# Chunk 0 of a state space scan moved in front of the last two blocks of an input projection

## The chip, the cores and the metric

One core of a Trainium2 chip runs the whole kernel in one launch. The metric is the device time of one execution in microseconds (us). Engines are named as in the profile: PE is TensorE's matmul, PEld its weight load, DVE VectorE, ACT ScalarE, POOL GpSimd, SP SyncE, whose queue issues all the DMAs here.

## The reference

One decoder block on 1024 tokens of width 1024, in float32:

```
h    = LN(x)
proj = h @ w_in                      # 5648 columns: xs 1024, z 1024, B 256, C 256, dt 16, glu 2048, cgate 1024
xbc  = silu(causal conv of width 4 over (xs, B, C));   dt = softplus(dt + bias)
y    = ssd(xs, dt, B, C) + d_skip * xs                 # 16 heads of 64, 2 groups, state 128, chunks of 128 tokens
yz   = y * silu(z);   y_ssm  = yz * rsqrt(mean(yz^2) per group) * norm_g
u    = glu_a * sigmoid(glu_b);  u = silu(LN(causal conv of width 31 over u));  y_conf = u * silu(cgate)
h    = LN(alpha * h + concat(y_ssm, y_conf) @ w_out + b_out)
out  = LN(alpha * h + sigmoid(h @ w_gate) * (p @ w_ple))
```

In the scan, each chunk of 128 tokens has a part within the chunk, (C B^T masked and decayed) times (dt * xs), and from chunk 1 on a part that reads the state left by the chunks before it, C times state. Then the state is decayed and the chunk's own B^T (decayed dt * xs) is added.

## The kernel before, in words

All large products are done as three products of two-part numbers (a rounded high part and the rest), accumulated in one PSUM bank: `three`, L122 to 125. A weight or activation is split in two by `split` (L117): ACT casts the high part, another engine (mostly POOL) subtracts it for the low part.

The input projection works in blocks of 128 output columns: `inproj` (L188) makes 48 products of 128x512 for a block, 24 a half, into banks "ps" of the PSUM tag "s" (three banks), each half emptied by ACT. The blocks come in the order: dt, B, C and xs beside the conformer's glu blocks (L624 to 633), then z blocks (`z_tile`, L384, output `zt`, stored to `z_d`), then eight gate blocks (`gate_tile`, L294, output `cg`), whose results are multiplied into the conformer's `accs` and stored to `mix_d`; the last two z blocks, z6 and z7, stand behind them (LAST_Z = 2, L636 to 641).

`prep(c)` (L441) prepares a chunk: it loads `xb` (xs, B and C of the chunk), the decay rows `gt` twice and `ea`, takes 16 exps on ACT, transposes xs on PE (`xtok`) for `xdt` (DVE) and `xdd` (ACT), transposes B and forms C B^T (`bps`), masks it (`cbm`) and multiplies it into the decay (L477). `chunk(c)` (L485) makes `yo` (C times state, not for chunk 0), `yd` (the part within the chunk), adds the skip into `y` on DVE, multiplies by `sz` (silu of z, loaded from `z_d` by `z_load`), stores `y_d`, and moves the state on with `sp` (L514 to 521). `mean_square(c)` (L524) squares `y` into the buffer of `ea` and sums it (`pr`). `conf_out(c)` (L548) is the conformer half of the output projection for the chunk's 128 tokens: 48 products into two banks "pso" (tag "o"), in the order of the weights wc[0] to wc[7], with the two parts `mH`, `mL` that `mix_load(c)` made. The weights `wc` are loaded and split by `out_weight` (L419): raw `wor`, high part `woh`, low part `wol`; wc[3] and wc[7] put `wor` in a "y" buffer (L644). The other half of the output projection (`out_proj`, "pss") and the gate (`gate`, "psg") follow for all chunks at the end.

Buffers are shared by tag: "xb" 2, "gt" 4, "u" 2, "xd" 2, "y" 2, "ha" 3, "st" 1 (L67), and areas "W" 8, "E" 4, "M" 4, which hold the two parts of h (`hH`, `hL`) until the last block of the input projection has read them. In code order the "y" buffers go to cg of gate blocks 0, 1, 6, 7, to zt of z6 and z7, to wor of wc[3] and wc[7], then to y of chunk 0, 1 and so on; the "xb" buffers to xb(0), mraw of mix_load(0), xb(1), xb(2).

The order on each engine's queue is not written by hand. The framework's planner fixes it before the run from the order of the code, the dependences, the buffers and its own estimate of each instruction's time; the engines then run their queues in that order, each waiting for semaphores.

The part around the change, before:

```
ready = [prep(0)]                                        # L635
while len(others) > LAST_Z: others.pop(0)()              # z2 to z5
for j in range(NK): gate_tile(j, CG_TAGS[j])             # gate blocks 0 to 7
for f in others: f()                                     # z6, z7
wc = [...]; mix = [mix_load(0)]; szs = [z_load(0)]       # L644
ready.append(prep(1)); szs.append(z_load(1))
for c in range(NT):                                      # L650
    done = chunk(c, szs.pop(0), *ready.pop(0))
    ...                                                  # prep(c + 2), mean_square(c), mix_load(c + 1), conf_out(c)
```

Of the kernel before, what the change touches and what calls it, by code (L numbers as in the profile page):

```python
# [15 lines left out]
L = 1024  # L16
# [30 lines left out]
def tile_block(ctx: ExitStack, tc: tile.TileContext, x, pT, wple, win, wdt, wout, wgate, vec, rows, heads, out):  # L47
# [22 lines left out]
    def work(name, tag, n=L):  # L70
        return wk.tile([P, SIZE.get(tag, L)], F32, name=name, tag=tag, bufs=BUFS[tag])[:, 0:n]

    def slabs(a, n=NK):
        return a.rearrange("p (k l) -> p k l", k=n)

    def bank(name):
        return pp.tile([P, 512], F32, name=name, tag="s", bufs=3)
# [68 lines left out]
    def area(name, tag):  # L146
        return regA.tile([P, L], F32, name=name, tag=tag, bufs={"W": 8, "E": 4, "M": 4}[tag])
# [146 lines left out]
    def gate_tile(j, tag):  # L294
        cg = work("cg", tag)
        inproj(T_CG + j, lambda hs, ps: nc.scalar.activation(out=cg[:, hs], in_=ps, func=AF.Silu))
        nc.scalar.activation(out=accs[j], in_=accs[j], func=AF.Silu, scale=v("clg", j), bias=v("clb", j))
        nc.vector.tensor_tensor(out=accs[j], in0=accs[j], in1=cg, op=ALU.mult)
        nc.sync.dma_start(out=mix_d[:, :, j, :].rearrange("t p l -> p t l"), in_=by_chunk(accs[j]))
# [141 lines left out]
    def prep(c):  # L441

        xb = slabs(work("xb", "xb", 12 * P), 12)
        nc.sync.dma_start(out=xb, in_=xbc_d[c])
        gg = []
        for g in range(2):
            gt = slabs(work("gt", "gt"))
            r0 = c * HEADS + g * 8
            nc.sync.dma_start(out=gt, in_=acs_d[r0:r0 + 8, :].unsqueeze(0).broadcast_to([P, 8, P]))
            gg.append(gt)  # L450
        ea = slabs(work("ea", "u") if c == 0 else area("ea", "E"))
        for q in range(2):
            er = ea_d[c * HEADS:(c + 1) * HEADS, :].rearrange("(t q) l -> q t l", q=2)[q]
            nc.sync.dma_start(out=ea[q * HD:(q + 1) * HD], in_=er.unsqueeze(0).broadcast_to([HD, NK, P]))

        for h in range(HEADS):
            sl = gg[h // 8][:, h % 8, :]
            nc.scalar.activation(out=sl, in_=sl, func=AF.Exp, bias=col(nacs, c, h))
        xdt = work("xdt", "xd")
        xt = pair("xtok")  # L460
        for t in range(NK):
            nc.tensor.transpose(out=xt[:, t * P:(t + 1) * P], in_=xb[:, t, :], identity=ident)
        nc.vector.tensor_tensor(out=heads3(xdt), in0=heads3(xt), in1=col(dtok, c, 0, HEADS).unsqueeze(2).broadcast_to([P, HEADS, HD]), op=ALU.mult)
        xdd = work("xdd", "u") if c == 0 else area("xdd", "E")
        for h in range(HEADS):
            nc.scalar.activation(out=xdd[:, h * HD:(h + 1) * HD], in_=xdt[:, h * HD:(h + 1) * HD], func=AF.Copy, scale=col(dec, c, h))
        bps = bbank("bps")
        for g in range(2):
            nc.tensor.transpose(out=bps[:, g * P:(g + 1) * P], in_=xb[:, 8 + g, :], identity=ident)
            mm(bps[:, (2 + g) * P:(3 + g) * P], lhsT=xb[:, 8 + g, :], rhs=xb[:, 10 + g, :], start=True, stop=True)  # L470
        btok = wk.tile([P, 2 * P], F32, name="btok", tag="btok")
        nc.scalar.copy(out=btok, in_=bps[:, 0:2 * P])
        cbm = wk.tile([P, 2, P], F32, name="cbm", tag="cbm", bufs=1)
        nc.vector.tensor_tensor(out=cbm, in0=bps[:, 2 * P:4 * P].rearrange("p (g l) -> p g l", g=2),
                                in1=tri.unsqueeze(1).broadcast_to([P, 2, P]), op=ALU.mult)
        for g in range(2):
            nc.vector.scalar_tensor_tensor(out=gg[g], in0=gg[g], scalar=1.0, in1=cbm[:, g:g + 1, :].broadcast_to([P, 8, P]), op0=ALU.min, op1=ALU.mult)  # L477
        return xb, gg, ea, xdt, xdd, btok

    def z_load(c):  # L480
        sz = slabs(work("sz", "xd" if c == 0 else "u"))
        nc.sync.dma_start(out=sz, in_=z_d[c])
        return sz

    def chunk(c, sz, xb, gg, ea, xdt, xdd, btok):  # L485
        y = slabs(work("y", "y"))
        for g in range(2):

            ys = y[:, g * 4:g * 4 + 4, :]
            es = ea[:, g * 4:g * 4 + 4, :]  # L490
            if c:
                yo = bank("yo")
                for t in range(4):
                    j = g * 4 + t
                    mm(yo[:, t * P:(t + 1) * P], lhsT=state[:, j * P:(j + 1) * P], rhs=xb[:, 10 + g, :], start=True, stop=True)
                nc.vector.tensor_tensor(out=es, in0=slabs(yo, 4), in1=es, op=ALU.mult)
            yd = bank("yd")
            for h in range(8):
                q = h % 2
                t = h // 2  # L500
                hh = g * 8 + h
                mm(yd[q * HD:(q + 1) * HD, t * P:(t + 1) * P], lhsT=xdt[:, hh * HD:(hh + 1) * HD], rhs=gg[g][:, h, :], start=True, stop=True)
            for t in range(4):
                j = g * 4 + t
                nc.vector.scalar_tensor_tensor(out=y[:, j, :], in0=xb[:, j, :], scalar=v("dsk", j), in1=yd[:, t * P:(t + 1) * P], op0=ALU.mult, op1=ALU.add)
            if c:
                nc.gpsimd.tensor_tensor(out=ys, in0=ys, in1=es, op=ALU.add)
        nc.gpsimd.tensor_tensor(out=y, in0=y, in1=sz, op=ALU.mult)
        nc.sync.dma_start(out=y_d[c], in_=y)
        if c + 1 < NT:  # L510
            if c:
                nc.gpsimd.tensor_tensor(out=heads3(state), in0=heads3(state),
                                        in1=col(cdec, c, 0, HEADS).unsqueeze(2).broadcast_to([P, HEADS, HD]), op=ALU.mult)
            for g in range(2):  # L514
                sp = bank("sp")
                gs = slice(g * 512, g * 512 + 512)
                mm(sp, lhsT=btok[:, g * P:(g + 1) * P], rhs=xdd[:, gs], start=True, stop=True)
                if c:
                    nc.vector.tensor_tensor(out=state[:, gs], in0=state[:, gs], in1=sp, op=ALU.add)
                else:  # L520
                    nc.vector.tensor_copy(out=state[:, gs], in_=sp)
        return y, ea

    def mean_square(c, y, ea):  # L524

        sq = ea.rearrange("p (g t) l -> p g t l", g=2)
        nc.scalar.activation(out=sq, in_=y.rearrange("p (g t) l -> p g t l", g=2), func=AF.Square)
        nc.gpsimd.tensor_tensor(out=sq[:, :, 0:2, :], in0=sq[:, :, 0:2, :], in1=sq[:, :, 2:4, :], op=ALU.add)
        nc.gpsimd.tensor_tensor(out=sq[:, :, 0, :], in0=sq[:, :, 0, :], in1=sq[:, :, 1, :], op=ALU.add)
        pr = bbank("pr")  # L530
        for g in range(2):
            mm(pr[:, g:g + 1], lhsT=sq[:, g, 0, :], rhs=inv512[:, 0:1], start=True, stop=True)
        rsm = const.tile([P, 2], F32, name=f"rsm{c}")
        vem = small("vem", 2)
        nc.vector.tensor_scalar(out=vem, in0=pr[:, 0:2], scalar1=EPS, scalar2=None, op0=ALU.add)
        nc.gpsimd.tensor_tensor(out=rsm, in0=vem, in1=mhalf[:, 0:2], op=ALU.pow)
        rss.append(rsm)

    def mix_load(c):
        raw = slabs(work("mraw", "xb", L) if c == 0 else area("mraw", "M"))  # L540
        nc.sync.dma_start(out=raw, in_=mix_d[c])
        ha = work("ha", "ha")
        nc.sync.dma_start(out=ha, in_=ha_d[c])
        mH, mL = slabs(area("mH", "M")), slabs(area("mL", "M"))
        split(raw, mH, mL, nc.gpsimd if c else nc.vector)
        return mH.bitcast(F32R), mL.bitcast(F32R), ha
# [88 lines left out]
    ready = [prep(0)]  # L635
    while len(others) > LAST_Z:  # L636
        others.pop(0)()
    for j in range(NK):
        gate_tile(j, CG_TAGS[j])
    for f in others:  # L640
        f()

# [1 line left out]
    wc = [out_weight(wout[NK + k], *regs[k], "y" if k % 4 == 3 else None) for k in range(NK)]  # L644
    mix = [mix_load(0)]
    szs = [z_load(0)]
    ready.append(prep(1))
    szs.append(z_load(1))
    ws = []
    for c in range(NT):  # L650
        done = chunk(c, szs.pop(0), *ready.pop(0))
        if c + 2 < NT:
            ready.append(prep(c + 2))
            szs.append(z_load(c + 2))
        mean_square(c, *done)
        if c + 1 < NT:
            mix.append(mix_load(c + 1))
        conf_out(c, *mix.pop(0))
        if c < 3:
            ws.append(out_weight(wout[c], area, "W", None, v("sng", c)))  # L660
# [72 lines left out]
```

## Time and profile before

| | us |
|---|---|
| median of 3 runs (lowest, highest) | 900.91 (900.71, 906.92) |
| the profiled execution | 904.0 |
| its span, first to last instruction | 902.3 |

The profile is that of the one profiled execution; times in it count from the first instruction. Its mean granted TensorE clock is 0.994 of full. Times of rows are us unless marked ns; L12 is line 12 of the kernel. A busy time of PE is modelled at its end, so the number of products in a stretch says more than their durations do.

### The profile page before, as it was taken

The page shows a single profiled execution, that of the slowest core. Times are in us where ns is not written, and L with a number is a line of the kernel's source. Part 1 is how long each engine was busy: PE and PEld are TensorE (multiplying, and loading weights), DVE is VectorE, ACT ScalarE, POOL GpSimd, SP SyncE. Part 2 cuts the span into 40 slices and gives each one's busy share as a digit, 9 for nine tenths or more (in the row PEclk, how much of TensorE's full clock was granted, in tenths as well). Part 3 has the DMA queues.
Part 4 walks back from the last instruction along what each step waited for, and adds up shares of the span by engine and source line. Part 5 has one row for each costly group of instructions (what it writes and reads, how often), then busy time and mean ns, then how long its engine had stood idle before and what let it go on. Part 6 is the DMA issues. An engine that isn't in the chain of part 4 may idle for free. (4 is left out here: it accounts for less than half of the span.)

```text
span 902.3 us, 11012 instructions
## 1 busy us (share of the span) xinstructions
PE 866.7 (96%) x4141; PEld 705.7 (78%) x4141; DVE 638.4 (71%) x738; ACT 393.5 (44%) x649; POOL 515.2 (57%) x298
## 2 busy tenths in 40 slices
PE   6989999999999999999999999999999889999995
PEld 4757888888888888888788887777877668888885
DVE  7968993799999989894414604774664876666666
ACT  4632336767334456554584536754743421111001
POOL 2559829999832299997652345666666432222211
PEclk9999999999999999999999999999999899999999
DMA  9612423121221313234241879787787702222211
GB/s 339 252 44 97 176 84 117 30 94 46 94 84 58 94 46 129 70 94 117 70 141 47 249 232 338 268 305 224 250 274 262 291 24 94 94 94 93 71 47 70
DMA packets 67716, 126.42 MB, mean 140 GB/s; under 512 B 4176, under 2 KB 41552, under 8 KB 67664
## 3 DMA queue, kind: packets, MB, share of 16 engines
q1 hardware_dynamic: 67664, 125.73, 41.5%
q8 instruction: 32, 0.52, 0.2%
q14 instruction: 20, 0.16, 0.1%
HBM read 89.93 MB, written 35.78 MB: 139 GB/s over the span
## 5 line engine op out<-in xcount | busy, mean ns | idle before, releaser
L123 PE MATMUL ps<-hH,wl 128*128 128x512 f32 x704 | 274.4, 391 | 2.5 <-DVE hH L177 2.5
L124 PE MATMUL ps<-hL,wh 128*128 128x512 f32 x704 | 274.8, 391 | 1.1 <-DVE hL L179 1.1
L125 PE MATMUL ps<-hH,wh 128*128 128x512 f32 x704 | 274.3, 390 | 0.0
L291 DVE SCALAR_TENSOR_TENSOR pc<-u,vc,pc 128x1024 f32<-128x1024 f32 x174 | 223.7, 1285 | 3.5
L286 POOL TENSOR_TENSOR acc<-acc,prod 128x1024 f32<-128x1024 f32 x60 | 146.1, 2435 | 18.1 <-ACT acc L282 15.3
L123 PEld LDWEIGHTS ps<-hH,wl 128*128 128x128 f32 x704 | 131.9, 188 | 29.8 <-DVE hH L177 3.0
L124 PEld LDWEIGHTS ps<-hL,wh 128*128 128x128 f32 x704 | 132.3, 188 | 28.9 <-DVE hL L179 1.5
L125 PEld LDWEIGHTS ps<-hH,wh 128*128 128x128 f32 x704 | 132.3, 188 | 27.4 <-issue 0.2
L120 POOL TENSOR_TENSOR wl<-wraw,wh 128x1024 fp32r<-128x1024 f32 x44 | 110.2, 2504 | 72.6 <-PE ps L123 39.1
L132 POOL TENSOR_SCALAR ve<-mv 128x1 f32<-128x1 f32 x24 | 22.2, 926 | 122.1 <-DVE mv L612 86.9
L285 ACT ACTIVATE prod<-u,vc 128x1024 f32<-128x1024 f32 x60 | 69.0, 1153 | 46.8 <-POOL acc L286 36.7
L119 ACT CAST wh<-wraw 128x1024 fp32r<-128x1024 f32 x44 | 46.2, 1049 | 67.8 <-DMA wraw<-in_win_dram 42.5
L380 DVE SCALAR_TENSOR_TENSOR pc<-xin,vc,pc 128x512 f32<-128x512 f32 x72 | 53.5, 747 | 5.9 <-ACT pc L247 3.4
L123 PE MATMUL pss<-woh,yL 128*128 128x512 f32 x128 | 51.7, 404 | 5.7 <-DVE r L581 3.5
L123 PE MATMUL pso<-woh,mL 128*128 128x512 f32 x128 | 51.8, 407 | 2.9 <-POOL mL L120 1.9
L123 PE MATMUL psg<-woh,hTL 128*128 128x512 f32 (+1 forms) x136 | 52.3, 385 | 1.1 <-DVE hTL L120 1.1
L125 PE MATMUL psg<-woh,hTH 128*128 128x512 f32 (+1 forms) x136 | 52.0, 382 | 0.0
L125 PE MATMUL pso<-woh,mH 128*128 128x512 f32 x128 | 51.9, 407 | 0.0
L124 PE MATMUL pso<-wol,mH 128*128 128x512 f32 x128 | 51.7, 404 | 0.0
L124 PE MATMUL psg<-wol,hTH 128*128 128x512 f32 (+1 forms) x136 | 51.6, 380 | 0.0
L124 PE MATMUL pss<-wol,yH 128*128 128x512 f32 x128 | 50.9, 398 | 0.0
L125 PE MATMUL pss<-woh,yH 128*128 128x512 f32 x128 | 50.9, 398 | 0.0
(183 smaller groups left out, 1390.4 us busy)
## 6 DMA issues: line engine op xcount, KB each, us to landing
wraw<-in_win_dram SPq DMA_DIRECT2D x44, 512.0 KB, 3.7
gt<-acs_d SPq DMA_DIRECT2D x16, 512.0 KB, 5.2
wor<-in_wout_dram SPq DMA_DIRECT2D x16, 512.0 KB, 6.8
xbc_d<-cacc SPq DMA_DIRECT2D x12, 512.0 KB, 3.4
xb<-xbc_d SPq DMA_DIRECT2D x8, 768.0 KB, 6.3
xt<-in_x_dram SPq DMA_DIRECT2D x8, 512.0 KB, 8.9
ple_d<-pl SPq DMA_DIRECT2D x8, 512.0 KB, 3.8
ha_d<-xt SPq DMA_DIRECT2D x8, 512.0 KB, 4.8
```

The lines of the kernel that those rows point to most:

```text
L119: nc.scalar.copy(out=h.bitcast(F32R), in_=src)
L120: leng.tensor_tensor(out=l.bitcast(F32R), in0=src, in1=h, op=ALU.subtract)
L123: mm(ps, lhsT=ll, rhs=rh, start=first, stop=False)
L124: mm(ps, lhsT=lh, rhs=rl, start=False, stop=False)
L125: mm(ps, lhsT=lh, rhs=rh, start=False, stop=last)
L132: eng.tensor_scalar(out=ve, in0=var, scalar1=EPS, scalar2=None, op0=ALU.add)
L285: nc.scalar.activation(out=pr, in_=u[:, i:i + L], func=AF.Copy, scale=v("ccw", j * KC + i))
L286: nc.gpsimd.tensor_tensor(out=acc, in0=acc, in1=pr, op=ALU.add)
L291: nc.vector.scalar_tensor_tensor(out=pc if i + 1 < KC else acc, in0=u[:, i:i + L], scalar=v("ccw", j * KC + i), in1=pc, op0=ALU.mult, op1= ...
L380: nc.vector.scalar_tensor_tensor(out=pc, in0=xin[:, o + j:o + j + 512], scalar=v("scw", i * 4 + j), in1=pc, op0=ALU.mult, op1=ALU.add)
```

## The change

Behind the last gate block and ahead of z6 and z7, the code now has chunk 0 up to its `y`, the state after chunk 0 (`advance(0)`) and prep(1). The gating of chunk 0 by z, its store, and all of chunk 1 on stay behind the weights `wc` in the loop. `chunk` is cut in three: `chunk` (y), `gated` (times silu of z, and the store) and `advance` (the state). The buffers move with it: `ea` of chunk 0, never read for its values, is no longer loaded, and `mean_square(0)` takes an "E" area of its own; `ea(1)` and `xdd(1)` take "u" buffers in place of "E" areas, `sz(1)` an "xd" buffer in place of a "u" one, and `mraw` of mix_load(0) a "gt" buffer in place of an "xb" one. The `y` of chunk 0 now comes ahead of zt of z6 and z7 and of wor of wc[3] and wc[7] in the order of the "y" buffers.

```diff
@@ prep @@
-        ea = slabs(work("ea", "u") if c == 0 else area("ea", "E"))
-        for q in range(2):
+        ea = slabs(work("ea", "u") if c == 1 else area("ea", "E")) if c else None
+        for q in range(2 if c else 0):
...
-        xdd = work("xdd", "u") if c == 0 else area("xdd", "E")
+        xdd = work("xdd", "u") if c < 2 else area("xdd", "E")
@@ z_load @@
-        sz = slabs(work("sz", "xd" if c == 0 else "u"))
+        sz = slabs(work("sz", "xd" if c < 2 else "u"))
@@ chunk @@
-    def chunk(c, sz, xb, gg, ea, xdt, xdd, btok):
+    def chunk(c, xb, gg, ea, xdt):
...
-            es = ea[:, g * 4:g * 4 + 4, :]
             if c:
+                es = ea[:, g * 4:g * 4 + 4, :]
...
+        return y
+
+    def gated(c, y, sz):
         nc.gpsimd.tensor_tensor(out=y, in0=y, in1=sz, op=ALU.mult)
         nc.sync.dma_start(out=y_d[c], in_=y)
+
+    def advance(c, xdd, btok):
+
         if c + 1 < NT:
...
-        return y, ea
@@ mean_square @@
+        if ea is None:
+            ea = slabs(area("sq", "E"))
@@ mix_load @@
-        raw = slabs(work("mraw", "xb", L) if c == 0 else area("mraw", "M"))
+        raw = slabs(work("mraw", "gt") if c == 0 else area("mraw", "M"))
@@ the order @@
     for j in range(NK):
         gate_tile(j, CG_TAGS[j])
+
+    y0 = chunk(0, *ready[0][0:4])
+    advance(0, *ready.pop(0)[4:])
+    ready.append(prep(1))
     for f in others:
         f()
...
     szs = [z_load(0)]
-    ready.append(prep(1))
     szs.append(z_load(1))
     ws = []
     for c in range(NT):
-        done = chunk(c, szs.pop(0), *ready.pop(0))
+        if c:
+            xb, gg, ea, xdt, *rest = ready.pop(0)
+            y = chunk(c, xb, gg, ea, xdt)
+        else:
+            y, ea = y0, None
+        gated(c, y, szs.pop(0))
+        if c:
+            advance(c, *rest)
         if c + 2 < NT:
             ready.append(prep(c + 2))
             szs.append(z_load(c + 2))
-        mean_square(c, *done)
+        mean_square(c, y, ea)
```

## Rows read from the trace of the kernel before

**Rows 1.** The page, busy us of the engines (share of the span), xinstructions.
```profile
PE 866.7 (96%) x4141; PEld 705.7 (78%) x4141; DVE 638.4 (71%) x738; ACT 393.5 (44%) x649; POOL 515.2 (57%) x298
```
**Rows 2.** Busy us by stretch: stretch, length, engines (xinstructions), PEclk, DMA share, GB/s.
```profile
521.00:543.00 22.00, 22.00 (x99) 18.19 (x97) 1.76 (x1) 7.59 (x10) 10.50 (x4) 1.00 0.69 216
...
543.00:575.00 32.00, 28.50 (x189) 22.73 (x188) 21.74 (x31) 23.82 (x61) 17.62 (x8) 1.00 0.94 309
575.00:699.00 124.00, 119.91 (x722) 95.50 (x721) 72.80 (x119) 62.62 (x182) 83.61 (x54) 1.00 0.80 266
...
688.00:699.00 11.00, 11.00 (x49) 9.09 (x50) 5.24 (x11) 4.31 (x4) 7.37 (x6) 1.00 0.87 327
...
705.00:710.00 5.00, 5.00 (x12) 3.33 (x11) 5.00 (x3) 1.04 (x1) 5.00 (x3) 0.50 1.00 366
```
**Rows 3.** Waits of PE, 543 to 699: us in total, times, longest.
```profile
PE bps L469 <- DVE cbm L474: 2.4, 1, 2.4
PE pr L532 <- POOL ea L529: 1.9, 2, 1.7
PE pso L123 <- POOL mL L120: 1.9, 1, 1.9
PE pso L123 <- DVE mL L120: 1.0, 1, 1.0
```
**Rows 4.** Timeline of PE: start, us, line, operation, tiles, count, [idle before <-releaser].
```profile
543.27 1.97 PE L502 MATMUL yd<-gt,xdt 128*64 128x128 f32 x32
545.28 1.13 PE L517 MATMUL sp<-xdd,btok 128*128 128x512 f32 x2
...
560.97 1.05 PE L495 MATMUL yo<-xb,state 128*128 128x128 f32 x8
561.86 1.04 PE L462 MATMUL xtok<-ident,xb 128*128 128x128 f32 x8
565.33 0.33 PE L469 MATMUL bps<-ident,xb 128*128 128x128 f32 x1 [2.44 <-DVE cbm L474]
...
704.53 0.79 PE L123 MATMUL pss<-woh,yL 128*128 128x512 f32 x1 [2.25 <-DVE ha L555]
```
**Rows 5.** Tile gt, 455 to 480: ns min/median/max, first and last start.
```profile
L458 ACT ACTIVATE gt<-gt,nacs x32: 384/387/405, 458.4 to 475.1; 128x128 f32<-128x128 f32 x32
```
**Rows 6.** Timeline of SP: DMA issues.
```profile
539.39 0.33 SPq L422 DMA_DIRECT2D wor<-in_wout_dram  x1
...
545.25 0.38 SPq L387 DMA_DIRECT2D z_d<-zt  x1
546.31 0.33 SPq L422 DMA_DIRECT2D wor<-in_wout_dram  x1
547.39 0.32 SPq L444 DMA_DIRECT2D xb<-xbc_d  x1
...
550.85 0.32 SPq L482 DMA_DIRECT2D sz<-z_d  x1
```
**Rows 7.** Waits of SP, 520 to 575.
```profile
SPq L422 <- DMA z_d<-zt: 5.8, 1, 5.8
...
SPq L444 <- DVE mL L120: 0.7, 1, 0.7
```
**Rows 8.** Tile zt, 521 to 556 (the stores of z6 and z7).
```profile
DMA to landing us min/median/max: 5.5/5.9/6.2
```
**Rows 9.** Tile wor, 500 to 575 (11 loads, ns of the casts).
```profile
L119 ACT CAST woh<-wor x8: 1046/1050/1054, 513.1 to 552.0; 128x1024 fp32r<-128x1024 f32 x8
...
DMA to landing us min/median/max: 3.3/6.8/11.6
```
**Rows 10.** Timeline of POOL, 550 to 562.
```profile
553.21 2.39 POOL L120 TENSOR_TENSOR wol<-wor,woh 128x1024 fp32r<-128x1024 f32 x1 [3.59 <-ACT woh L119]
559.14 2.40 POOL L508 TENSOR_TENSOR y<-y,sz 128x1024 f32<-128x1024 f32 x1 [3.54 <-DVE xdt L463]
561.49 2.37 POOL L120 TENSOR_TENSOR mL<-mraw,mH 128x1024 fp32r<-128x1024 f32 x1
```

## The prediction

> **What bounds the kernel now.** Read the busy line first: TensorE is busy 866.7 of 902.3 us, VectorE, the next, 638.4 [rows 1]. So the time is TensorE's work plus the little that it waits, and a reorder can only gain by removing waits. The table by stage comes second. In the last blocks of the input projection (521 to 543) TensorE is busy 22.00 of 22.00 us; from 543 to 575, where the state space part begins, 28.50 of 32.00; from 575 to 699, where it runs beside the output projection of the conformer half, 119.91 of 124.00 [rows 2]. So the stretch that the change leaves with less work has 3.5 us of idle TensorE, the rest of that part another 4.1, and the place that the work goes to has none. The list of waits names them: bps for cbm 2.4, pr for POOL's squares 1.9, pso for POOL's mL 1.9, pso for VectorE's mL 1.0 [rows 3]. They are single hand-overs, none over 2.5 us. The timeline of TensorE gives the pieces [rows 4], and the timeline of the DMA issues and the waits on SP what came late and why [rows 6, 7].
>
> **Two habits of the order that the trace shows.** The queues are not in the order of the code: 32 exps of decay tiles, two chunks' worth, run from 458.4 to 475.1 us, though the second chunk's preparation is written behind all gate and z blocks [rows 5]. The planner moves what is ready forward. But buffers of one tag are given out in the order of the code: xb of chunk 1 is issued at 547.39, once mraw of mix_load(0), which stands ahead of it under the same tag, has been split (SP waited 0.7 for that mL) [rows 6, 7]; and a wor load waited 5.8 us for a z_d store to land, because it takes that z block's "y" buffer [rows 7]. I carry both over.
>
> **The change, part by part.** Call T the end of the last z block (543.27 before).
>
> 1. Work moved. Chunk 0's 32 yd (1.97 us) and 4 sp (1.13 for two, so 2.3), and prep(1)'s 8 xtok (1.04) and 6 bps (8 xtok take 1.04, so 0.8) [rows 4]: 6.1 us of TensorE, now between gate block 7 and z block 6. None is added or removed: 0. T moves later by 6.1. In the new place they need PSUM banks of the "s" tag (three) that VectorE and ACT must have emptied. At least 0, with xtok and bps as filler between; at most about 2 us (sp waiting until VectorE, with the gate products ahead in its queue, has read yd). The row nearest is the 0 of idle in 521 to 543, where the same banks turn over; I take 0.4.
>
> 2. Waits removed. xb(1) no longer stands behind mraw(0) (which takes a "gt" buffer), ea(1) and xdd(1) no longer wait for the input projection's "E" area, so prep(1) is finished long before T. bps of chunk 2 waited 2.44 for cbm of chunk 1, because both preparations ran back to back [rows 4]: gone, -2.4. The 1.0 for mL(0) was left over after yd and sp of chunk 0; behind T now stand yo and yd of chunk 1 (2.1 + 2.0) and xtok and bps of chunk 2 (1.8), 5.9 against the 4.1 (547.42 less T) behind which mL(0) was there: gone, -1.0. If that cover is late, it stays. Sum -3.4; bounds 0 and -3.4 here, and -7.2 if chunk 1 being ahead also takes the two waits of 1.9.
>
> 3. A wait added. There are two "y" buffers. Before, they went to z6, z7, then wor of wc[3] (z6's, issued 539.39), wor of wc[7] (wc[3]'s, issued 546.31 when POOL had split it), y of chunk 0 (z7's) [rows 6]. Now y0 holds one from before z6 until it is gated, and it can't be gated before z7 is stored and read back. z6, z7, wor of wc[3] and wor of wc[7] go through the other, one after the other. So: z7's store is issued at T+2.0 (545.25) and landed at T+7.6 (sz of chunk 0, which waits for it, is issued at 550.85) [rows 6]; the two stores took 5.5 and 6.2 us [rows 8]. Then wor of wc[3]: loads of wor here took 3.3 to 11.6, median 6.8, with the DMA engines 0.94 busy [rows 2, 9]; prep(1)'s and most of prep(2)'s loads are out of the way now, so I take 4.5: T+12.1. Cast 1.05 [rows 9] and POOL's split 2.39 [rows 10]: ready at T+15.6, where before it was ready at T+3. wor of wc[7] again 4.5 + 1.05 + 2.39: T+23.6; before POOL's split of it ended at 555.6, T+12.3 [rows 10].
>
> TensorE until T+15.6: yo(1) 2.1, yd(1) 2.0, the 18 products of conf_out(0) with wc[0] to wc[2] at 11.00/49 = 0.224 us [rows 2] 4.0, sp(1) 2.3, xtok and bps of chunk 2 1.8, yo(2) 2.1: 14.3. Wait 1.3. Then wc[3] to wc[6], 24 products, 5.4, and yd(2) 2.0: T+23.0; wait 0.6. conf_out(0) ends near T+25; mL(1) needs its "M" buffer, so POOL's 2.37 [rows 10] and the hand-over stand behind that end, covered by xtok(3), bps(3) and sp(2), 4.1. In front of these waits the engine's queue is fixed, so what stands behind a product that waits can't be used as cover; before, 32 us of this stretch lost 3.5 though there was work. I take 2 more for that. Sum 1.3 + 0.6 + 2 = about +4. Bounds: 0 (all covered), and +9.8 if wor lands at the median 6.8 (ready at T+17.9) and only yo(1), yd(1) and the 18 products (8.1) stand ahead of wc[3].
>
> 4. SP and POOL. The gating of chunk 0 is behind z7's store as before; SP issues sz(0), sz(1) and the wor loads in a new order, but each still waits for the same landing. sz(1) and xdt(2) now share "xd" buffers with sz(0): xdt(2) can't be written before y0 is gated (T+7.6, a load of 4.5, POOL's 2.40 [rows 10]: T+14.5), and yd(2) is not needed before T+21. Hidden. Nothing here is an instruction more, but for no ea load of chunk 0 (its two DMAs fall away, far from any wait): 0.
>
> Sum: +0.4 - 3.4 + 4 = +1.0. The profiled execution spans 902.3 and took 904.0 with 1.7 around it; it would take 905.0. The median of the runs shown, 900.9, is 3.1 below the profiled one, so I forecast 902.0: no change. (A measurement of this kernel can tell about 1%, 9 us, from none.)
>
> [...]
>
> **Rivals.**
> - Slower: the "y" buffer decides. If the planner puts the product with wc[3] ahead of chunk 2's work, TensorE stands at it until T+17.9. It decides as soon as the work queued ahead of that product is under some 12 us. Price: 9.8, the clock 2.3, the new place up to 2, less 3.4: +8.7 to +10.7, 909.6 to 911.6. For it: 5.8 us that SP stood for a z_d store already before. Against: the planner found cover in most such places (124 us with 4.1 idle).
> - Faster: the chain is covered to the end, and the chunks, one ahead, no longer wait for POOL at the two places of 1.9: 0.4 - 7.2, 894.1. For it: the waits of the later part are all hand-overs between chunk and conf_out. Against: POOL is no less busy, and the lead is used up by the first long cover.
> - The change does nothing: the planner already moved half of prep(1) forward, and may keep chunk 0's products where they are. 900.9. Against: xb(1) was held by its buffer, and that is what changes.
>
> **How the numbers follow.** Forecast case 0.50 (899 to 906), slower rival 0.25, faster rival 0.20, nothing 0.05. Of the slower one about half lies over 909.9, and little of the faster one under 891.9: faster 0.05, within 1% 0.82, slower 0.13. The range goes from the faster rival's 894 to 913, the slower one's upper price and a little.
>
> **What would show it.** Right: yd of chunk 0 and xtok of chunk 1 in front of the last two z blocks, with TensorE's idle still near 0 there; no wait of bps for cbm after T; a wor load that waits for z7's store, and a pso product that waits for POOL's wol some 14 to 18 us behind T, and perhaps again 8 later. Wrong: no such wait of pso for wol, y0 gated before z7 ends, waits of TensorE over 3 us in 521 to 550, or the loss of whole microseconds behind 700, which I take as unchanged.

## The result and the profile after

The change made the kernel slower: 916.8 us (median of 4 runs, 914.85 to 919.2) against 903.59 for the kernel before (4 runs, the three shown ahead and one of 906.26), a ratio of 1.0121 with a 95% interval of 1.008 to 1.0162 (the two medians alone give 1.0146, inside that interval). The forecast was 902.0, no change, and its range ended at 913. The profiled execution took 916.33 us, its span is 914.6. A trace is of one execution, and the runs of the kernel before in the groups below reach from 899.35 to 913.01 us; a difference of a few us between two traces shows little by itself. One run of a variant below (mraw in an "ha" buffer, in the kernel before) took 1094.11 us at a granted clock of 0.752 and is left out of its median and ratio.

The busy line of the page comes first, as in [rows 1]:

```profile
PE 873.6 (96%) x4141; PEld 709.9 (78%) x4141; DVE 635.5 (69%) x738; ACT 397.0 (43%) x651; POOL 512.9 (56%) x298
```

TensorE has the same 4141 products and is busy 6.9 us longer (866.7 before). Of a span that grew by 12.3 us, 5.4 are new idle time; for the other 6.9 the same products are busy for longer, at a mean granted clock of 0.985 where it was 0.994. Where that lies shows when the span is cut at four events: the end of gate block 7, the end of z7 (T), the end of the last "pso" product, and the end.

| stretch | before, us | after, us | difference |
|---|---|---|---|
| start to the end of gate block 7 | 521.4 | 521.8 | +0.4 |
| chunk 0, its state, prep(1) | none | 8.6 | +8.6 |
| z6 and z7 | 21.8 | 21.9 | +0.1 |
| T to the last pso product | 155.8 | 155.0 | -0.8 |
| from there to the end | 203.3 | 207.3 | +4.0 |

The fourth line is the one to stop at. It lost 6.1 us of products to the second and should have become 149.7; it became 155.0. The stretches as the table by stage has them, in the kernel before (columns as in [rows 2], the engines in the order PE, PEld, DVE, ACT, POOL):

```profile
543.30:699.00 155.70, 148.11 (x908) 118.20 (x908) 94.54 (x149) 86.14 (x243) 101.23 (x61) 1.00 0.83 275
...
699.00:902.00 203.00, 187.97 (x861) 154.03 (x859) 138.90 (x167) 35.11 (x42) 56.42 (x43) 0.97 0.27 98
```

and in the changed one, with two short stretches behind them:

```profile
521.80:530.40 8.60, 5.90 (x51) 3.97 (x51) 3.96 (x10) 4.84 (x6) 5.64 (x2) 1.00 0.72 244
...
552.30:707.30 155.00, 146.24 (x858) 116.46 (x857) 82.80 (x136) 79.26 (x217) 98.73 (x61) 0.97 0.80 260
707.30:914.00 206.70, 189.26 (x861) 155.34 (x859) 138.57 (x167) 35.04 (x42) 56.72 (x43) 0.97 0.26 95
565.50:568.90 3.40, 2.88 (x4) 1.18 (x4) 1.16 (x2) 0.18 (x1) 2.82 (x2) 0.50 0.86 301
579.10:585.90 6.80, 5.12 (x28) 4.13 (x28) 3.55 (x12) 5.04 (x14) 6.25 (x5) 0.50 0.70 201
```

Behind T there are 50 products less (858 for 908), but TensorE is busy only 1.9 us less, and its mean granted clock went from 1.00 to 0.97. The last two lines say where: two stretches, 3.4 and 6.8 us long, at 0.50.

The waits of TensorE, in the place and up to the last pso product, and then behind it (us in total, times, longest):

```profile
PE sp L523 <- DVE ea L496: 3.9, 1, 3.9
PE yo L495 <- DVE y L505: 2.9, 1, 2.9
PE sp L523 <- ACT cg L296: 1.8, 1, 1.8
PE sp L523 <- DVE y L505: 0.9, 1, 0.9
...
PE psg L123 <- DVE hTL L120: 4.2, 1, 4.2
PE pss L123 <- DVE r L588: 3.7, 1, 3.7
PE pt L597 <- DVE r L575: 1.0, 1, 1.0
```

Against [rows 3]: the wait of bps for cbm (2.4) and the 1.0 for mL are gone, as forecast. In their place stand one of 3.9 and one of 2.9 behind T, and 1.8 and 0.9 in the new place. No product waits for wol by name. The timelines show how the two "y" buffers come into both long waits all the same. The DMA issues, then ACT (the first three lines belong to the new place), POOL, VectorE and TensorE:

```profile
555.37 0.37 SPq L387 DMA_DIRECT2D z_d<-zt  x1
561.41 0.33 SPq L422 DMA_DIRECT2D wor<-in_wout_dram  x1
...
570.52 0.38 SPq L422 DMA_DIRECT2D wor<-in_wout_dram  x1
```

```profile
523.64 1.05 ACT L119 CAST woh<-wor 128x1024 fp32r<-128x1024 f32 x1 [6.49 <-DMA wor<-in_wout_dram]
524.87 1.04 ACT L119 CAST woh<-wor 128x1024 fp32r<-128x1024 f32 x1 [0.18 <-DMA wor<-in_wout_dram]
525.82 0.59 ACT L296 ACTIVATE cg<-ps 128x512 f32<-128x512 f32 x1
...
559.98 2.45 ACT L458 ACTIVATE gt<-gt,nacs 128x128 f32<-128x128 f32 x8
...
564.63 1.05 ACT L119 CAST woh<-wor 128x1024 fp32r<-128x1024 f32 x1 [1.16 <-DMA wor<-in_wout_dram]
...
571.00 3.81 ACT L458 ACTIVATE gt<-gt,nacs 128x128 f32<-128x128 f32 x12 [0.18 <-DMA gt<-acs_d]
574.71 3.92 ACT L466 ACTIVATE xdd<-xdt,dec 128x64 f32<-128x64 f32 x16
578.53 1.04 ACT L534 ACTIVATE sq<-y 128x1024 f32<-128x1024 f32 x1
...
580.36 1.03 ACT L119 CAST woh<-wor 128x1024 fp32r<-128x1024 f32 x1
```

```profile
565.81 2.35 POOL L120 TENSOR_TENSOR wol<-wor,woh 128x1024 fp32r<-128x1024 f32 x1 [2.72 <-ACT woh L119]
568.42 2.37 POOL L511 TENSOR_TENSOR y<-y,sz 128x1024 f32<-128x1024 f32 x1 [0.27 <-DMA sz<-z_d]
...
582.80 2.36 POOL L120 TENSOR_TENSOR wol<-wor,woh 128x1024 fp32r<-128x1024 f32 x1
```

```profile
562.47 1.71 DVE L477 SCALAR_TENSOR_TENSOR gt<-gt,cbm 128x1024 f32<-128x1024 f32 x1 [4.23 <-ACT gt L458]
564.09 1.27 DVE L428 SCALAR_TENSOR_TENSOR wol<-wor,vc,woh 128x1024 fp32r<-128x1024 f32 x1
565.29 0.68 DVE L496 TENSOR_TENSOR ea<-yo,ea 128x512 f32<-128x512 f32 x1
...
579.61 2.15 DVE L505 SCALAR_TENSOR_TENSOR y<-xb,vc,yd 128x128 f32<-128x128 f32 x8 [2.89 <-ACT sq L534]
```

```profile
566.02 2.08 PE L523 MATMUL sp<-xdd,btok 128*128 128x512 f32 x2 [3.89 <-DVE ea L496]
...
569.51 0.79 PE L124 MATMUL pso<-wol,mH 128*128 128x512 f32 x1
...
580.78 2.07 PE L495 MATMUL yo<-xb,state 128*128 128x128 f32 x8 [2.91 <-DVE y L505]
```

Read them as one chain, with T = 552.3. z7's zt is issued to `z_d` at T+3.1. The load of wc[3], which needs z7's "y" buffer, goes out when that store has landed, at T+9.1. Cast at 564.63, split by POOL until 568.16: T+15.9. The load of wc[7] goes out at T+18.2. But its cast stands in ACT's queue behind 12 exps, 16 `xdd`, the square of y0 and three more exps, and runs at 580.36; the split ends at 585.16, T+32.9 (before: T+12.3). The other "y" buffer is no freer: `y` of chunk 1 (579.61) waits until ACT's square has read y0 out of it, and `yo` at 580.78 waits for that. Without wc[3] TensorE had 18 of the 48 products of conf_out(0) to do, and those were done by 558.9. What was left, at 562.1, was an `sp` that needs a bank that VectorE empties at 565.29, behind a decay product that waits for ACT's exps and behind a weight split. So the wait carries the name of `ea`; what had been taken away, by this reading, was the other work that would have stood there (the first experiment bears that out). SP's queue is not the difference: it stood at a wor load for a z_d store for 5.6 us, and for 5.8 before [rows 7]. conf_out(1) starts at 591.1 where before it started at 566.0.

### The profile page after: what moved, and what is told of

The parts are those of the page before. It is cut to its first block, busy times and chain, and to the rows that moved or that the text cites. A ratio compares the mean times of both kernels' runs of the same rounds, so it can differ in the third digit from the quotient of the medians.

```text
span 914.6 us, 11000 instructions
## 1 busy us (share of the span) xinstructions
PE 873.6 (96%) x4141; PEld 709.9 (78%) x4141; DVE 635.5 (69%) x738; ACT 397.0 (43%) x651; POOL 512.9 (56%) x298
## 4 chain that ended last, share of the span: by engine, by line
PE 78%; DMA 6%; DVE 5%; ACT 3%; POOL 3%; issue 2%; SPq 2%; POOLq 0%; DVEq 0%; ACTq 0%
PE ps L124 16%; PE ps L125 16%; PE ps L123 16%; PE psg L123 3%; PE psg L125 3%; PE psg L124 3%; PE pss L123 3%; PE pss L125 3%; PE pss L124 3%; PE pso L123 2%; PE pso L124 2%; PE pso L125 2%; DMA gt<-acs_d 1%; DMA yraw<-y_d 1%; DMA wor<-in_wout_dram 1%
## 5 line engine op out<-in xcount | busy, mean ns | idle before, releaser
L120 POOL TENSOR_TENSOR wol<-wor,woh 128x1024 fp32r<-128x1024 f32 x12 | 31.9, 2666 | 35.2 <-ACT woh L119 18.3
```

The lines of the kernel that those rows point to most:

```text
L120: leng.tensor_tensor(out=l.bitcast(F32R), in0=src, in1=h, op=ALU.subtract)
```

## The experiments

Ratios are to runs of the kernel before on the same chip; the medians of that kernel there were 905.26, 905.98 and 906.53 us in the three groups of runs. The quotients of the medians differ from these ratios by up to 0.1%.

**y0 out of the "y" buffers, in the changed kernel**

```diff
-        y = slabs(work("y", "y"))
+        y = slabs(work("y", "y" if c else "ha"))
```

> The changed kernel with one edit: y of chunk 0 takes an "ha" buffer (free since the gate blocks) in place of one of the two "y" buffers. Theory Y (y0 holds a "y" buffer, so the stores of z6 and z7 and the weights wc[3] and wc[7] pass one by one through the other, and y of chunk 1 waits for y0): the two long waits of TensorE behind the last z block (sp for ea 3.9, yo for y 2.9) go, and the half-clock stretches at 565 and 579 with them. From the end of z7 to the last pso product the changed kernel takes 154.9 us; expected 149 to 151; span 908 to 910, and 905 if the extra 4 us behind 707 come from the same lateness. Rival P (the place itself: without chunk 0 and prep(1) as cover, the part behind z7 waits whatever the buffers): still 154 to 156 and a span of 914 to 916.

Measured: 906.13 us, ratio 1.0003 (0.9974 to 1.0031). The loss of 1.2% is gone with this one word. The stretch from T to the last pso product in the table by stage:

```profile
550.50:696.40 145.90, 143.01 (x858) 114.48 (x857) 88.85 (x136) 78.38 (x216) 98.43 (x61) 1.00 0.83 275
```

The same 858 products take 145.9 us instead of 155.0, and the 9.1 split in two: idle 2.89 for 8.76, so 5.9 of waits, and busy 143.01 for 146.24, so 3.2 of clock (1.00 for 0.97). wc[7] is split at 560.98, T+10.5. It also shows what the wait of 3.9 was short of. Here the exps of that decay tile end later behind T (T+12.8) than in the changed kernel (559.98 and 2.45 above: T+10.1):

```profile
560.85 2.45 ACT L458 ACTIVATE gt<-gt,nacs 128x128 f32<-128x128 f32 x8
```

But TensorE doesn't stand for them. From 557.9 to 565.4 it works at the 30 products of wc[3] to wc[7], which in the changed kernel's queue stand behind the late wc[3].

What the kernel doesn't get is a gain. The wait of pss for `r` became 7.7, and from the last pso product to the end it takes 207.6 (203.3 before).

**The buffer alone, in the kernel before.** Nothing is moved but the moment at which y0 takes its "y" buffer: a write by POOL, one element in each partition, claims it in front of z6.

```diff
+    y_first = slabs(work("y", "y"))
+    nc.gpsimd.memset(y_first[:, 0, 0:1], 0.0)
     for f in others: f()
...
-        y = slabs(work("y", "y"))
+        y = y_first if c == 0 else slabs(work("y", "y"))
```

> The kernel before, order and all, with one edit: y of chunk 0 takes its "y" buffer where the changed kernel takes it (in front of z6, by a tiny write of POOL) and holds it until it is gated; chunk 0 itself stays behind z7. Theory Y (the buffer alone costs the time): end of z7 at 542 to 543 as before, from there to the last pso product 163 to 167 us in place of 155.8 (the 9.2 that giving y0 another buffer won back in the changed kernel), span 909 to 914. Rival P (it takes the moved work too): 155 to 157, span 902 to 904.

Measured: 916.18 us, ratio 1.0123 (1.0094 to 1.0151). That is the whole loss of the change (1.0121), with all the work in its old place. Its stretch behind T, and its waits there:

```profile
541.60:705.10 163.50, 151.00 (x908) 120.45 (x908) 91.92 (x150) 85.60 (x242) 97.99 (x60) 0.98 0.83 262
```

```profile
PE xtok L462 <- DMA xb<-xbc_d: 5.2, 3, 3.9
PE pso L124 <- POOL wol L120: 2.6, 1, 2.6
PE yo L495 <- DVE state L519: 2.5, 1, 2.5
PE sp L517 <- DVE state L519: 1.4, 1, 1.4
```

163.5 against 155.8 before, with the 908 products of before: 7.7 us, of which 4.9 are idle time (12.50 for 7.59) and 2.9 clock. Here the planner laid the queue in another order, and the waits are for xb, for wol by name, and for the state; that all of them come from the same shortage is likely, but no run separates them. The rest of the loss lies behind: from the last pso product to the end it takes 207.3, for 203.3 before.

**prep(1) put back behind z7, in the changed kernel**

```diff
     advance(0, *ready.pop(0)[4:])
-    ready.append(prep(1))
     for f in others: f()
...
     szs = [z_load(0)]
+    ready.append(prep(1))
```

> The changed kernel with the preparation of chunk 1 put back behind z7; chunk 0 and its state stay in front of z6. Theory: the loss hangs on the buffer of y of chunk 0, which is still taken in front of z6 here, so it stays: ratio 1.007 to 1.017, and from the end of z7 to the end of the conformer half 155 to 161 us (155.0 in the changed kernel, plus at most the 1.8 of preparation that comes back). Rival: the preparation in front was what left TensorE without cover behind z7, and with its 1.8 us and its loads back there, the wait for the weights is covered: that stretch 150 to 153 and a ratio of 0.998 to 1.004.

Measured: 921.19 us, ratio 1.0172 (1.0125 to 1.0218); 162.4 us from T to the last pso product. The loss stays and is somewhat larger, just over both bounds of the theory and far from the rival's 0.998 to 1.004. The cover that prep(1) took along isn't what is missing. The wait that leads the list behind T:

```profile
PE xtok L462 <- DVE xdt L463: 7.8, 1, 7.8
```

It is one wait in place of two: xtok of chunk 2 needs a bank that VectorE empties for xdt of chunk 1, and that stands in VectorE's queue behind a decay product waiting for exps.

**The moved buffers without the move.** All of the change's edits to buffers and functions, but chunk 0, its state and prep(1) called where they stood before, so that the order of the "y" buffers is the old one.

```diff
-    y0 = chunk(0, *ready[0][0:4])
-    advance(0, *ready.pop(0)[4:])
-    ready.append(prep(1))
     for f in others: f()
...
     szs = [z_load(0)]
+    ready.append(prep(1))
     szs.append(z_load(1))
...
         else:
-            y, ea = y0, None
+            xb, gg, ea, xdt, *rest = ready.pop(0)
+            y = chunk(c, xb, gg, ea, xdt)
         gated(c, y, szs.pop(0))
-        if c:
-            advance(c, *rest)
+        advance(c, *rest)
```

> The changed kernel's buffers (no ea load for chunk 0, ea(1) and xdd(1) in "u", sz(1) in "xd", mraw(0) in "gt", squares of chunk 0 in an "E" area) in the order of the kernel before: chunk 0, its state and prep(1) stand behind z7 again. If the order costs the time, this is at the kernel before or better: the wait of bps for cbm (2.4) is gone, span 899 to 902. If the moved buffers cost it (xdt(2) and sz(1) sharing "xd"), span 906 or more.

Measured: 908.62 us, ratio 1.0041 (1.0009 to 1.0072). About a third of the size of the loss. The profiled span is 908.7, so by the expectation the moved buffers cost something of their own. Two waits lead the list between T and the last pso product:

```profile
PE sp L523 <- ACT zt L386: 3.4, 1, 3.4
PE xtok L462 <- DMA xb<-xbc_d: 2.5, 2, 1.5
```

With the work in front and y0 elsewhere (the first experiment) the first isn't on the list, the second is 0.4, and the ratio is 1.0003: this cost doesn't add to the buffer's.

**mraw of mix_load(0) out of the "xb" buffers, in the kernel before**

```diff
-        raw = slabs(work("mraw", "xb", L) if c == 0 else area("mraw", "M"))
+        raw = slabs(work("mraw", "ha") if c == 0 else area("mraw", "M"))
```

> The kernel before with one edit: mraw of mix_load(0) takes an "ha" buffer in place of an "xb" one, so xb of chunk 1 can be loaded long ahead. If the only thing the change could win is that xb(1) came late, this wins it alone: the wait of bps for cbm (2.4) goes, span 899 to 901. Rival: the wait turns into another of the same size (VectorE's xdt(1) waits for an "xd" buffer until chunk 0 is done): 902 to 903.

Measured: 902.78 us, ratio 0.9964 (0.9938 to 0.999). xb of chunk 1 no longer stands behind that buffer, and T to the last pso product takes 152.7 (155.8 before). The wait of bps for cbm is gone; in part another has come in its place, 1.9 of xtok of chunk 2 for its xb. Part of what the change was good for is to be had by one buffer, without moving anything.

**The state products of chunk 0 in the other PSUM banks, in the changed kernel**

```diff
-                sp = bank("sp")
+                sp = bank("sp") if c else obank("sp0")
```

> The changed kernel with one edit: the two sp products of chunk 0 go to banks of the PSUM tag "o" (free there) in place of "s". Theory B (between gate block 7 and z6 the moved work takes 8.5 us for about 6 of products, since sp waits 1.8 for ACT to empty the gate block's bank and 0.9 for VectorE's y): 6 to 6.5 us there, end of z7 at 550 in place of 552.3, span 912 to 913. Rival: the wait only passes to the next user of an "s" bank (the first half of z6), end of z7 still at 552, span 914 to 916.

Measured: 915.62 us, ratio 1.0107 (1.005 to 1.0164). The new place:

```profile
521.60:526.90 5.30, 5.30 (x51) 4.04 (x51) 0.10 (x1) 2.59 (x3) 1.75 (x1) 1.00 0.93 318
```

5.3 us without idle time, 3.3 less than the 8.6 of the change: the waits there were for banks of the tag "s". The first of them was ACT's emptying of gate block 7 (525.82 in ACT's lines above), which stood behind two casts of weights, the first of which had waited 6.49 us for its load. Of the 3.3 us nothing can be told at the end: the interval holds the ratio of the change, and T to the last pso product becomes 161.3 (in a profiled run that was the slowest of the four).

**That edit and y0's, in the changed kernel**

```diff
+        y = slabs(work("y", "y" if c else "ha"))
...
+                sp = bank("sp") if c else obank("sp0")
```

> The changed kernel with y0 in "ha" and the two sp products of chunk 0 in "o" banks. The place between gate block 7 and z6 took 7.9 us with y0 in "ha" alone, 5.3 with sp in "o" alone: 5.3 expected here. With the y buffers out of the way this reaches the end: span 901 to 902, 2 to 3 less than with y0 in "ha" alone (904.0). Rival: the part behind z7 is bound by its own chain of loads and splits, so an earlier end of z7 only lengthens the waits behind it: 904.

Measured: 906.53 us, ratio 0.9995 (0.9969 to 1.0021). The place takes 5.3 us, T to the last pso product 149.7, the rest 206.3. So also without the buffer's chain an earlier T is not carried through. The longest wait left is the 6.3 of pss for `r`, and the next edit goes for it.

**And the low part of y of chunk 1 split on POOL** (on top of the two edits just shown)

```diff
-        split(raw, yH, yL, nc.vector if c < 2 else nc.gpsimd)
+        split(raw, yH, yL, nc.vector if c < 1 else nc.gpsimd)
```

> As the kernel with y0 in "ha" and sp in "o", and the second split of y for the output projection (yL of chunk 1) on POOL in place of VectorE. With y0 in "ha" alone, TensorE waited 7.7 us at 702 for r of the output projection, which stood in VectorE's queue behind that split, and the split behind a load of y. Theory Q (VectorE's queue order is what gives the gain back): that wait falls to about 2, the half clock behind it to nothing or 3 us, span 896 to 899. Rival (the loads and splits of the last weights bound it, whichever engine): the wait passes to the next product, span 901 to 904.

Measured: 900.59 us, ratio 0.9939 (0.9914 to 0.9964): 0.6% below the kernel before. The profiled span is 900.3, where 896 to 899 was expected. From the first pss to the first psg product it takes 31.1 us (35.9 without this edit, 32.9 before). VectorE's timeline shows what went; first without the edit, then with it:

```profile
703.99 3.28 DVE L120 TENSOR_TENSOR yL<-yraw,yH 128x1024 fp32r<-128x1024 f32 x1 [3.49 <-DMA y_d<-y]
707.19 3.36 DVE L428 SCALAR_TENSOR_TENSOR wol<-wor,vc,woh 128x1024 fp32r<-128x1024 f32 x1
710.47 0.74 DVE L588 SCALAR_TENSOR_TENSOR r<-pss,rsm,r 128x512 f32<-128x512 f32 x1
```

```profile
703.63 2.48 DVE L428 SCALAR_TENSOR_TENSOR wol<-wor,vc,woh 128x1024 fp32r<-128x1024 f32 x1 [3.23 <-ACT woh L427]
706.03 0.74 DVE L588 SCALAR_TENSOR_TENSOR r<-pss,rsm,r 128x512 f32<-128x512 f32 x1
```

`r`, which empties the first pss banks, stood behind a split that waited for the store of the last y (`y_d<-y`; VectorE stood idle for it for 3.49 us, until 703.99). It is not the load of y that the expectation named: the low part yL of chunk 1 goes into a "y" buffer (L568), and the last y gives that buffer up when it is stored. So this wait, too, is one for the two "y" buffers. With that split on POOL, `r` runs 4.4 us earlier, and the wait of pss for it falls from 6.3 to 2.2.

**The last edit alone, in the kernel before**

```diff
+        split(raw, yH, yL, nc.vector if c < 1 else nc.gpsimd)
```

> The kernel before with one edit: the low part of y of chunk 1 is split on POOL, not on VectorE, as in the combined variant that came out at 0.9939 [0.9914, 0.9964]. Theory: that variant's gain is this edit alone (0.9939 against 0.9995 without it), and the work in front of z6 has no part in it. Then this run has a ratio of 0.992 to 0.997, and the stretch from the first pss product to the first psg product, 32.9 us before, falls to some 31. Rival: the edit helps only where chunk 0 is out of the way; with the changed mraw buffer and chunk 0 behind z7 it moved nothing (0.9979 against 0.9964). Then the ratio is 0.998 to 1.002 and that stretch stays at 32 to 34.

Measured: 904.59 us, ratio 0.9982 (0.9953 to 1.0011), and 32.8 us from pss to psg. The rival was right: alone the edit does nothing that can be told from none.

```profile
PE pss L123 <- DVE r L581: 4.9, 1, 4.9
```

**The last edit with mraw's, in the kernel before**

```diff
+        raw = slabs(work("mraw", "ha") if c == 0 else area("mraw", "M"))
...
+        split(raw, yH, yL, nc.vector if c < 1 else nc.gpsimd)
```

> The kernel before with mraw of mix_load(0) in "ha" and yL of chunk 1 on POOL. With mraw in "ha" alone the stretch behind z7 took 152.7 in place of 155.8, and the way from the first product of the output projection to the first of the gate 35.3 in place of 32.9, with a wait of 5.0 for r. Theory Q: that wait falls to about 2, span 897 to 899. Rival: 901 to 903.

Measured: 904.36 us, ratio 0.9979 (0.9958 to 1.0). The wait for `r` stayed at 4.3. So the split on POOL pays in the version in which chunk 0 is out of the way, and not here; why the wait stays in these two wasn't followed further.

## Why the prediction was wrong

- **Step 3, the wait added, is the one that failed.** The chain through the buffer was right: wc[3] ready at T+15.6, measured T+15.9. That it fits so well is luck in part, as z7's store landed at T+9.1 and not T+7.6, and the load behind it took 3.2 us and not 4.5. How the chain would reach TensorE was not right: the sign that the prediction names, a pso that waits for wol, does not appear in the changed kernel. Its price was taken as +4, between bounds of 0 and 9.8; it is 9.1 by the first experiment (155.0 less 145.9) and 7.7 by the buffer held alone, each from one trace. The span was to grow by 1.0 and grew by 12.3; of the 11.3 between, 5.1 are this step, 4.0 the stretch behind 700, 2.1 step 1, -0.4 step 2, and 0.5 the stretches ahead of T. The traces show three things that the sum of step 3 lacks; none was priced by itself. First, wc[7] was put at T+23.6 by adding a landing, a cast and a split; the cast stood in ACT's queue behind exps, xdd and a square, and wc[7] came at T+32.9, so conf_out(0) ended at T+35.8 and not at T+25. Second, `y` of chunk 1 is on the same two buffers and was left out of the chain: it waited for the square of y0. Third, 14.3 us of work were counted as cover ahead of wc[3]; the fixed order used 9.8 of them and then came to an `sp` that waited 3.9.
- **The clock** is in no step of the sum; the slower rival's price has it, at 2.3 us. That is the loss of one stretch of the kernel before, from 705 to 710 at 0.50: 12 products took 5.00 us [rows 2], where 0.224 each makes 2.7. For the waits behind T no run shows that 2.3; there it was 3.2 in the changed kernel (busy 146.24 for 143.01) and 2.9 with the buffer held alone (151.00 for 148.11). At the ends of the two long waits, 3.89 and 2.91, the granted clock was 0.50; in the kernel before it stayed at 1.00 through a wait of 2.44 [rows 4].
- **Step 2, the waits removed, was right.** The waits for cbm and mL are gone. Forecast -3.4 against the 149.7 that were left; without the buffer's chain the stretch took 145.9, so -3.8. But it was given back behind: the first experiment has a ratio of 1.0003.
- **Step 1, the new place,** was taken at +0.4, at most 2; it cost 2.5 (8.6 for 6.1). ACT emptied the last half of gate block 7 no earlier in the kernel before (525.10, behind casts that had waited 6.09 us for a load; 525.82 in the changed one). But there z6 came next, which takes a new bank only after the 24 products of a half; here the two yd take two banks in 2 us and sp asks for the third. So the row chosen as the nearest was not near. This is a miss of the term, not the cause of the loss: two experiments made the place 5.3 us long and the time did not follow.
- **Step 4, SP and POOL at nothing:** y0 was gated by T+18.5, not T+14.5, and xdt of chunk 2 came at T+19.8. No wait of TensorE goes by it in the changed kernel.
- **"The loss of whole microseconds behind 700, which I take as unchanged"** was wrong: +4.0. The waits there went from 6.3 in all (for r 3.5, for ha 2.3, for hTL 0.5) to 8.9 (hTL 4.2, r 3.7, r 1.0), and busy time by 1.3. The experiments show VectorE's queue behind it in one place, `r` behind the split of y; they don't show why the change made it worse. It is not the buffer's chain: this stretch takes 205.0 to 208.1 us in eight of the ten variants, also in the first experiment (207.6 at a ratio of 1.0003) and with only mraw moved (208.1 at 0.9964). The two others are the one with all three edits (201.6) and the last edit alone in the kernel before (203.2). The prediction gives no row for taking it as unchanged.
- **The rival "the 'y' buffer decides"** is what happened. It was priced at 909.6 to 911.6 on 900.9, a ratio of 1.010 to 1.012, for a measured 1.0121 (by the medians +8.7 to +10.7 us for +13.2); it got a chance of 0.25. Its picture of TensorE standing at the product with wc[3] is not what the trace shows, so the close number is luck in part. The case against it, that the planner had found cover in most such places, rested on a stretch in which all the weights were there to be used as cover. The range ended at 913 and the runs at 916.8; 2.7 of this gap's 3.8 us are the base, as the median of the kernel before is 903.59 with its fourth run and not 900.91.

## What to carry to other kernels

When work moves forward, list every later user of each buffer that it takes, in code order, and give the whole list its new dates, with the queue of each engine on the way and not only the durations: here four tiles and one later y shared two buffers. Here the cover for a wait was work whose inputs had arrived, so the late weight also took away the cover for other hand-overs, and the waits carried other names. Two cheap tests settle such a case: give the moved tile a buffer of its own, and, in the kernel before, only claim the buffer early.

## What the runs showed of the hardware that was not expected

- In the changed kernel the granted clock fell to 0.50 while TensorE still stood in its waits of 3.89 and 2.91 us, and stayed there for 2.9 and 5.1 us after their ends (stretches 565.5 to 568.9 and 579.1 to 585.9). Behind T this came to 3.2 us beside 5.9 us of waiting. The length of one wait does not tell it. In the kernel before, the clock was at 0.50 for the last 0.6 us of a wait of 2.25 that ended at 704.53, and at 1.00 all through those of 2.44 [rows 4] and 2.26 (ended at 728.30). In the changed kernel it was at 1.00 through the 4.25 us that ended at 742.63, and at 0.50 from 743.0 to 746.4, behind them.
- The same weight split on VectorE (L428, 128x1024) took 1.27 us at 564.09 of the changed kernel and 3.30 at 713.02 of it (3.36 at 707.19 of the variant with y0 and the state's banks moved). Counted at its short time it is off by 2 us. POOL was idle beside the first and in two weight splits of its own beside the second (5.96 us from 712.59). In the traces of the kernel before and the changed one, between 540 and 760 us, the five such splits with POOL idle beside them took 1.27 to 1.28 us, and each of the five that took over 2 us (2.52 to 3.32) had POOL busy for at least 1.4 us of it. One with POOL busy beside it for 1.1 us took 1.28 (698.30 of the changed kernel). That POOL slows them was not tested.
